# Row sums of a 64 MB array on Trainium2: the first load takes half a row instead of one

## The chip, the cores and the metric

The kernel runs on one core of a Trainium2 chip. The time is device time in microseconds of one execution, from the runs' own clock; where several runs are given, their median stands. The engines that matter are VectorE (DVE in the profile) and ScalarE (ACT), which add, and SyncE (SP), which issues every transfer. The transfers themselves are carried out by 16 DMA engines.

## The reference

```
batch, seq, dim = 32, 512, 1024
x = np.random.randn(batch, seq, dim).astype(np.float32)

def reference(x):
    return np.sum(x, axis=-1).astype(np.float32)
```

There are 32 x 512 = 16384 rows of 1024 floats, 67.1 MB in all. The result is one float for each row, 64 KB.

## The kernel before

**Tiling.** The rows are cut into three blocks that give each of the 128 partitions 32, 48 and 48 consecutive rows (`BLOCKS`, line 10). Within a block, a partition's rows lie one behind the other in memory, so a load of 16 rows is 64 KB of consecutive bytes for every partition. The list `groups` (lines 80 to 88) has seven groups of 16 rows each, 8 MB a group, and the last 16 rows of the last block are loaded in smaller pieces: 9, 4 and 2 rows (`CUTS`) and then the very last row in two parts, of 544 and 480 columns, into the tensor `tail`.

**Buffers.** Three buffers `xt0` to `xt2` (line 37) hold 16 rows for each partition. Group b goes to buffer b modulo 3, and its landing counts on the semaphore `slot0`, `slot1` or `slot2`.

**Loads.** The list `loads` (lines 91 to 101) has every load in its order: buffer, destination, source, semaphore. Group 0 is loaded by two: row 0 with the semaphore `first`, rows 1 to 15 with `slot0` (line 93). Lines 135 to 138 issue them on SP's queue. From group 3 on, SP waits before the issue until VectorE has finished the group that had the buffer before (`freed`).

**Early loads.** At the end (lines 163 to 182) the first two loads (`EARLY`) are taken out of the kernel's body and put into the entry block of SP's program, ahead of the barrier with which all engines start. These are the two loads of group 0.

**Sums.** VectorE waits for `first` (line 106) and then, for each group, for its slot (line 109). `rows_dve` (line 55) is one reduction over 16 rows. In the last group ScalarE takes 7 of the rows (`rows_act`, line 64), and in the pieces about half. The last row is summed by `pairs_dve` (line 72): the two halves of a part are added and accumulated in one instruction.

**Stores.** When the body is done, SP stores three blocks of sums early, and the last 16 columns after the last sum (lines 139 to 147).

Of the kernel before, what the change touches and what calls it, by code (L numbers as in the profile page):

```python
# [11 lines left out]
BUFS = 3  # L12
ACT_ROWS = 7
CUT = 544
CUTS = (0, 9, 13, 15)
EARLY = 2


def row_sums(nc, x: bass.AP, out: bass.AP):
    P = nc.NUM_PARTITIONS  # L20
    x_flat = x.flatten_outer_dims()
    R, D = x_flat.shape
# [4 lines left out]
    xs, outs = [], []  # L27
# [6 lines left out]
    def sbuf(name, n):  # L34
        return nc.alloc_sbuf_tensor(name, [P, n], F32)

    xt = [sbuf(f"xt{i}", G * D) for i in range(BUFS)]
# [9 lines left out]
    sems = {n: nc.alloc_semaphore(n) for n in names}  # L47
    slots = [sems[f"slot{i}"] for i in range(BUFS)]
# [32 lines left out]
    for k, n in enumerate(BLOCKS):  # L81
        c = 0
        end = n - G if k == len(BLOCKS) - 1 else n
        while c < end:
            m = min(G, end - c)
# [4 lines left out]
    freed = {}  # L90
    loads = []
    for b, (k, c, m) in enumerate(groups):
        parts = [(0, m, slots[b % BUFS])] if b else [(0, 1, sems["first"]), (1, m, slots[0])]
        for i, j, s in parts:
            loads.append((b, xt[b % BUFS][:, i * D : j * D], xs[k][:, (c + i) * D : (c + j) * D], s))
    last = xt[n_bufs % BUFS]
    for k, (i, j) in enumerate(zip(CUTS, CUTS[1:])):
        loads.append((n_bufs, last[:, i * D : j * D], x_z[:, (z0 + i) * D : (z0 + j) * D], sems[f"piece{k}"]))
# [18 lines left out]
    for k in range(2):  # L117
        i, j = CUTS[k], CUTS[k + 1]
# [36 lines left out]
def kernel(tc: tile.TileContext, x: bass.AP, out: bass.AP):  # L155
    tc.close()
    tc.compile()  # L157
    nc = tc.nc
    row_sums(nc, x, out)

    sp = mybir.EngineType.SP
    fn = nc.m.functions[0]
    entry, body = None, None
    for blk in fn.blocks:
        ops = [i for i in blk.instructions if i.engine == sp]
        if entry is None:
            entry = blk
        elif any(i.opcode == "DMACopy" for i in ops):  # L170
            body = blk
            break
    code = list(body.instructions)
    loads = [i for i in code if i.engine == sp and i.opcode == "DMACopy"][:EARLY]
    for load in loads:
        assert not load.sync_info.on_wait
        code.remove(load)
    body.instructions = code
    code = list(entry.instructions)
    at = next(k for k, i in enumerate(code) if i.engine == sp and i.opcode == "Drain")  # L180
    code[at:at] = loads
    entry.instructions = code
# [29 lines left out]
```

## Time and profile before

| What | Value |
|---|---|
| Time, median of 3 runs | 160.74 us (160.47 to 160.75) |
| Profiled execution, its own time | 160.68 us |
| Span of that execution in the profile | 159.3 us |
| VectorE busy | 121.4 us |
| ScalarE busy | 17.2 us |
| DMA packets, bytes | 2448, 67.18 MB |
| Mean rate over the span | 422 GB/s |
| One reduction of 16 rows on VectorE | 17.2 us |

Times in the profile count from the start of the span, which is the issue of the first load. A "packet" is what one DMA engine moves at once; here it is one partition's consecutive bytes in one load, and each load has 128 of them, 8 for each of the 16 engines, plus one packet of 4 bytes for each engine that counts on the semaphore. The windows' rates count a packet where it starts, so in short windows with large packets they swing widely; in the first 2 us, where packets are 4 KB, they can be read directly. The difference of 1.4 us between the span and the time of the execution lies before the first and after the last recorded instruction.

### The profile page before, as it was taken

To read this page: it belongs to the slowest core of one execution; us is meant where nothing else is said; L and a number is where in the kernel's file an instruction comes from. 1 tells how busy PE (TensorE), PEld (TensorE's weight loads), DVE (VectorE), ACT (ScalarE), POOL (GpSimd) and SP (SyncE) were. 2 spreads that over 40 slices of the span, in tenths; PEclk is the share of its full clock that TensorE was granted. 3 is DMA by queue.
4 is the path that set the end of the run, shared out by engine and by line. 5 is a ranking of instruction groups with operands and counts; after the bars stand their busy time and mean duration, and the time that the engine had idled before them with its cause. 6 is when DMAs were issued, how large, how long until landed. Compare 5 with 4: busy or idle time off the path is not lost.

```text
span 159.3 us, 109 instructions
## 1 busy us (share of the span) xinstructions
DVE 121.4 (76%) x16; ACT 17.2 (11%) x31; POOL 0.2 (0%) x4
## 2 busy tenths in 40 slices
DVE  0000059998699968999599994999949999499785
ACT  3000000000000000000000000000000000394694
POOL 0000000000000000000000000000000000000000
DMA  9988996996996999979969969969969989699994
GB/s 378 494 386 355 494 526 263 526 510 280 526 494 296 526 395 395 526 329 461 526 280 510 526 263 526 510 280 526 494 296 526 428 362 526 296 444 444 391 409 138
DMA packets 2448, 67.18 MB, mean 422 GB/s; under 512 B 784, under 2 KB 912, under 8 KB 1168
## 3 DMA queue, kind: packets, MB, share of 16 engines
q1 hardware_dynamic: 2448, 67.18, 98.1%
HBM read 67.11 MB, written 0.07 MB: 422 GB/s over the span
## 4 chain that ended last, share of the span: by engine, by line
DMA 75%; DVE 22%; SPq 1%; issue 0%
DMA xt<-in_x_dram 50%; DMA tail<-in_x_dram 25%; DVE res L56 22%; SPq L138 1%; DVE pairs L74 0%; DVE res L74 0%
## 5 line engine op out<-in xcount | busy, mean ns | idle before, releaser
L56 DVE TENSOR_REDUCE res<-xt 128x16 f32<-128x16384 f32 (+3 forms) x9 | 119.8, 13309 | 34.1 <-DMA xt<-in_x_dram 34.1
L67 ACT ACTIVATE xt<-xt 128x1024 f32<-128x1024 f32 x15 | 15.6, 1042 | 138.2 <-DMA xt<-in_x_dram 138.2
L67 ACT ACTIVATION_READ_ACCUMULATOR xt<-xt 128x1 f32 x15 | 2.8, 186 | 0.0
L104 DVE MEMSET tail<- 128x1 f32 x1 | 0.1, 59 | 2.0 <-PEq L157 2.0
L67 ACT ACT_TABLE_LOAD x1 | 1.3, 1283 | 1.9 <-PEq L157 1.9
L74 DVE CUSTOM_DVE_ANT_0 pairs<-tail 128x272 f32<-128x272 f32 (+1 forms) x2 | 0.9, 427 | 0.2 <-DMA tail<-in_x_dram 0.2
L74 DVE CUSTOM_DVE_ANT_0 pairs<-xt 128x512 f32<-128x512 f32 x1 | 0.7, 692 | 0.2 <-DMA xt<-in_x_dram 0.2
L74 DVE DVE_READ_ACCUMULATOR2_ANT res<- 128x1 f32 x2 | 0.2, 82 | 0.0
L196 POOL MEMSET const-bfloat16-1.0<- 128x1 bf16 x1 | 0.1, 102 | 0.0
L196 POOL MEMSET const-uint8-127<- 128x1 uint8 x1 | 0.1, 102 | 0.0
L196 POOL MEMSET const-float32-1.0<- 128x1 f32 x1 | 0.1, 99 | 0.0
L196 POOL MEMSET const-float32-0.0<- 128x1 f32 x1 | 0.1, 98 | 0.2 <-issue 0.2
L74 DVE DVE_READ_ACCUMULATOR2_ANT tail<- 128x1 f32 x1 | 0.1, 83 | 0.0
## 6 DMA issues: line engine op xcount, KB each, us to landing
xt<-in_x_dram SPq DMA_DIRECT2D x1, 7680.0 KB, 21.3
xt<-in_x_dram SPq DMA_DIRECT2D x1, 4608.0 KB, 32.4
xt<-in_x_dram SPq DMA_DIRECT2D x1, 2048.0 KB, 36.9
xt<-in_x_dram SPq DMA_DIRECT2D x1, 1024.0 KB, 38.9
xt<-in_x_dram SPq DMA_DIRECT2D x1, 512.0 KB, 3.5
tail<-in_x_dram SPq DMA_DIRECT2D x1, 272.0 KB, 39.1
tail<-in_x_dram SPq DMA_DIRECT2D x1, 240.0 KB, 39.2
xt<-in_x_dram SPq DMA_DIRECT2D x6, 40.8
```

What stands on the lines that cost most here:

```text
L56: nc.vector.tensor_reduce(out=res[:, c : c + n], in_=t[:, j * D : (j + n) * D].rearrange("p (j d) -> p j d", d=D), axis=X, op=ADD,).then_i ...
L67: nc.scalar.activation(out=v, in_=v, func=COPY, accum_out=res[:, c + i : c + i + 1]).then_inc(act, 1)
L74: nc.vector.tensor_tensor_reduce(out=pairs[:, 0 : h - a], in0=t[:, a:h], in1=t[:, h:b], scale=1.0, scalar=0.0, op0=ADD, op1=ADD, accum_out ...
L104: nc.vector.memset(tail[:, CUT + 15 : CUT + 16], 0.0).then_inc(vec, 1)
L138: nc.sync.dma_start(out=dst, in_=src).then_inc(s, 16)
L196: nc = _bacc.Bacc("TRN2", target_bir_lowering=False, num_devices=1)
```

## The change

A constant `LEAD` of 512 columns is added, and the two loads of group 0 are cut there: the first one brings columns 0 to 511 of row 0 (2 KB for each partition, 256 KB in all) with the semaphore `first`, and the second one brings the rest of row 0 and rows 1 to 15 (62 KB for each partition) with `slot0`. To that end the list's bounds are counted in columns and no longer in rows. All other loads have the same bounds as before.

```
+LEAD = 512
...
     for b, (k, c, m) in enumerate(groups):
-        parts = [(0, m, slots[b % BUFS])] if b else [(0, 1, sems["first"]), (1, m, slots[0])]
+        parts = [(0, m * D, slots[b % BUFS])]
+        if b == 0:
+            parts = [(0, LEAD, sems["first"]), (LEAD, m * D, slots[0])]
         for i, j, s in parts:
-            loads.append((b, xt[b % BUFS][:, i * D : j * D], xs[k][:, (c + i) * D : (c + j) * D], s))
+            loads.append((b, xt[b % BUFS][:, i:j], xs[k][:, c * D + i : c * D + j], s))
```

## The prediction

> **What bounds the kernel now.** I read the page first, its chain and its queue above all, because they say which resource is last. Columns of the transfer rows: size of one, microseconds from issue to landing.
>
> ```profile
> span 159.3 us, 109 instructions
> DVE 121.4 (76%) x16; ACT 17.2 (11%) x31; POOL 0.2 (0%) x4
> q1 hardware_dynamic: 2448, 67.18, 98.1%
> DMA 75%; DVE 22%; SPq 1%; issue 0%
> L56 DVE TENSOR_REDUCE res<-xt 128x16 f32<-128x16384 f32 (+3 forms) x9 | 119.8, 13309 | 34.1 <-DMA xt<-in_x_dram 34.1
> xt<-in_x_dram SPq DMA_DIRECT2D x1, 7680.0 KB, 21.3
> xt<-in_x_dram SPq DMA_DIRECT2D x1, 512.0 KB, 3.5
> ```
>
> The 16 DMA engines are busy for 98.1% of the span; VectorE waits 34.1 us for loads. The 22% that the chain gives to VectorE is buffers being handed back, and that is no stall of the stream: the fourth load is issued when the first reduction ends (39.1 us), while the third load is still in flight until 60 us. So I asked next how evenly the stream runs, by stretches (columns: length, busy time of three engines, clock, share of the 16 DMA engines, GB/s):
>
> ```profile
> 0.90:1.40 0.50, 0.00 (x0) 0.00 (x0) 0.00 (x0) 1.00 0.93 197
> 1.40:1.90 0.50, 0.00 (x0) 0.00 (x0) 0.00 (x0) 1.00 0.90 254
> 1.90:2.40 0.50, 0.06 (x1) 0.49 (x1) 0.00 (x0) 1.00 0.90 360
> 21.00:117.00 96.00, 86.10 (x5) 0.00 (x0) 0.00 (x0) 1.00 1.00 431
> 0.90:157.40 156.50, 120.97 (x14) 17.20 (x31) 0.00 (x0) 1.00 1.00 429
> 155.25:156.50 1.25, 1.04 (x2) 1.25 (x3) 0.00 (x0) 1.00 1.00 386
> ```
>
> From 0.9 to 157.4 us the engines have no hole. The slow stretch is the first microsecond: busy by the record, but at half the rate. The change touches this stretch alone. The queue's own view, cut to two windows that both begin at 0.9 us and end at 1.9 and 2.4 us (packets, MB; share of 16 engines), and the issue of the first two loads on SP's queue (start, length):
>
> ```profile
> q1 hardware_dynamic: 55, 0.23, 91.5%
> ...
> q1 hardware_dynamic: 99, 0.41, 91.1%
> ```
>
> ```profile
> 0.00 0.37 SPq L138 DMA_DIRECT2D xt<-in_x_dram  x1
> ...
> 0.42 0.42 SPq L138 DMA_DIRECT2D xt<-in_x_dram  x1
> ```
>
> The first 55 packets (one is one partition's 4096 bytes) took 0.915 x 16 x 1.0 / 55 = 0.266 us each. The next 44 took (0.911 x 16 x 1.5 - 14.64) / 44 = 0.164 us. The start costs 55 x 0.102 / 16 = 0.35 us per engine, and it is over by about 1.9 us.
>
> **The change part by part.** The number of loads, packets, semaphores and waits stays; SP issues the same two loads first, and nothing is moved past another queue. VectorE waits for `first` and then for `slot0` before its first reduction, as before. That wait ends with the larger load (19.8 us of idle), so an earlier `first` starts nothing. Three costs are left.
>
> 1. Steady price of the packets. Between 60 and 96 us, 233 packets of 64 KB fill 97.9% of 16 engines: 2.420 us each. Against 0.164 us for 4 KB, a byte costs (2.420 - 0.164) / 61440 = 36.7 ps, 2 KB cost 0.075 us, and the rest of a packet is a constant of about 0.014 us. A 2 KB packet is then 0.089 us. The tail's loads (2176 and 1920 bytes per partition), 229 data packets in the 1.25 us that run at 386 GB/s, give 0.995 x 16 x 1.25 / 229 = 0.087 us, so the line holds at this size. Each engine saves 8 x 0.075 = 0.60 us in the first load and pays 8 x 0.075 = 0.60 us in the second one, whose packets grow from 60 to 62 KB. Eight and eight packets remain: sum 0.00 us.
>
> 2. The slow start. Is its 0.35 us charged by the packet, by the byte, or by the clock? If it is a sum for each of the first 55 packets, the same 55 pay it: 0.00. If it is a stretch of time that ends at 1.9 us, packets of 0.089 + 0.102 = 0.191 us let 14.64 / 0.191 = 77 start where 55 did, and 22 x 0.102 / 16 = +0.14 us. If the early packets last 0.266 us whatever their size, 55 of them move half the bytes: 55 x 0.075 / 16 = +0.26 us, and were that to hold for all 128 packets, first-load time would be 128 x 0.266 / 16 = 2.13 us where 55 x 0.266 + 73 x 0.164 over 16 is 1.66; less 0.60 us of bytes taken out, a loss of +1.07. On the other side, an excess in proportion to the packet's size halves: -0.17; and if larger packets following sooner absorbed all of it, -0.35. I take 0.00, between these, because the row of 0.164 us shows that the second half of the row already runs at full rate: the half that is taken out is not the half that suffers.
>
> 3. Cover for the second load. Nothing is free in the first load: its data keep the engines busy until the second load's packets can start. Now the first 60 KB packets start at 2.44 us (the queue's view from 2.4 us on); with 0.60 us less to move, the earliest engine would ask at 1.84. The first load's bytes begin 1.0 us after its issue; the same delay from 0.42 gives 1.42, within the 0.3 us over which engines start, 1.42 to 1.72. The upper bound that the trace allows is 2.44, since it only shows that they could start by then: a hole of up to 0.60 us. I take none, because the delay of the sister load, on the same queue with the same 128 partitions, is the nearest row. Were the cover gone, all 0.60 us would show at the end, since the stream has no hole afterwards in which to catch up.
>
> A rule of the Trainium skill speaks against the change: "DMA: Bandwidth & Descriptors", section "Rules for kernel authors", wants at least 1 MiB in a DMA for full bandwidth, and the new first load has a quarter of that. The trace does not show the loss where a queue is full: the tail's loads of 272 and 240 KB ran at 386 GB/s with the engines 100% busy. By that page's fitted price (section "Bandwidth", 2.0 us plus bytes at 436 GB/s, stated for another issuing path) both cuts sum to the same 4.0 us plus the same bytes, so even the rule gives no difference unless the second fixed part loses its cover. The same page's first-byte latency of about 0.6 us would have the second load ready at 1.02; the trace's own load took 1.0 us.
>
> The end is untouched: the last tail load lands at 157.44, one VectorE operation of 0.41 us and the last store follow. Span and the 1.4 us around it stay. The profiled execution took 160.68 us, 0.06 below the median of 160.74; a sum of 0.00 is 160.7, and I put it at the median, 160.75.
>
> **The rivals.** About 0.2% (0.32 us) is what a measurement of this kernel can tell from no change: the three runs lie 0.28 us apart.
>
> - A hole after the first load (slower). Price min(0.60, time ready - 1.84); it decides beyond the bound when the second load's packets can start only after 2.16 us. For it: each of the neighbouring issues on SP takes 0.37 to 0.42 us and the third and fourth loads are issued at 1.9 and 2.3, so what lies between an issue and its first packet may take longer for a load that follows another closely than the first load alone shows. Against it: 1.42 by the sister load. Time: 160.74 + 0.45 = 161.2 in the middle, 161.34 at most.
> - Early packets at a fixed latency (slower, or just inside the bound): half the bytes in flight, +0.26 us for the first 55 packets, 161.0; if more packets than these stay slow, +0.4 to +1.07. For it: busy engines at half rate, which is what latency with few bytes in flight looks like. Against: nothing shown of smaller packets at the start.
> - The start gets cheaper (faster). The end follows the slowest engine, and the engines do not start alike: the last 4 KB packet starts at 2.97 us, where 60 KB packets began at 2.44, so one engine is 0.5 us behind the first, and nothing later lets it catch up. If the excess goes with the bytes of the first load, the slowest engine has most to gain: -0.35 in the mean, up to -0.5: 160.4 to 160.2.
> - The transfer is hidden anyway: reordering bytes between two back-to-back loads changes nothing, and only the draw of which engine is late moves the time, by about the 0.28 us of the runs. This is the forecast itself.
>
> **How the numbers follow.** No change, cost of the start per packet or short of the bound: 0.44, time 160.6 to 161.0. A hole: 0.17, and a fixed latency or long slow stretch beyond the bound: 0.15; together slower 0.32. A cheaper start: 0.24. I give slower more than faster since its ends reach further (+0.60 and +1.07 against -0.5). The range leaves out the far ends, 0.08 on each side: 160.25 to 161.3. The likeliest case's own range is 160.55 to 160.95.
>
> **What would show it.** Right: 2448 packets again; the second load's first packets near 1.84 us with a full share in the windows on both sides; the 62 KB load landing about 21.3 us after its issue; `tail` landing at 157.4. Step 1 wrong: GB/s between 3 and 21 us differing by more than the shifted bytes. Step 2 wrong: mean packet time in 0.9 to 1.9 us far from 0.19 us. Step 3 wrong: a share of the DMA engines well under 0.9 in a window between 1.7 and 2.5 us, with the landing of the second load and of `tail` later by the same amount. Faster would show as the second load and `tail` landing earlier by equal amounts. What would make the forecast wrong is a start that is charged differently from packet to packet than one trace can show.

## The result and the profile after

The changed kernel takes 160.89 us in the median, the kernel before 160.69 us in the same comparison: a ratio of 1.0015, 95% interval 1.0009 to 1.0021. By that ratio it is 0.24 us more (the medians lie 0.20 us apart), below the 0.2% that the prediction took as its bound; the interval reaches 0.21%. In a second comparison (experiment 5) the ratio was 1.0006, interval 0.9997 to 1.0015, which takes in no change. The two intervals share 0.09 to 0.15%, or 0.14 to 0.24 us.

The page of the changed kernel, its transfer rows with size and microseconds from issue to landing:

```profile
span 159.3 us, 109 instructions
q1 hardware_dynamic: 2448, 67.18, 98.1%
DMA 75%; DVE 22%; SPq 1%; issue 0%
xt<-in_x_dram SPq DMA_DIRECT2D x1, 7936.0 KB, 21.4
xt<-in_x_dram SPq DMA_DIRECT2D x1, 256.0 KB, 2.7
```

Packets, bytes and the share of the DMA engines are those of before. The first load lands 0.8 us sooner after its issue (2.7 instead of 3.5 us), the second one 0.1 us later (21.4 instead of 21.3). Nobody gains from the earlier first landing, as VectorE's first reduction begins at 21.88 us instead of 21.83. The chain of the changed kernel (start, length) shows the same stream:

```profile
1.91 39.22 DMA xt<-in_x_dram
41.15 17.23 DVE res L57
...
118.32 39.10 DMA tail<-in_x_dram
157.42 0.04 issue
157.46 0.41 DVE pairs L75
```

The last load of this execution lands at 157.42 us; before it was 157.44. The profiled execution took 160.67 us and is the fastest of the changed kernel's runs, so it can't show the 0.24 us in its end. It does show what happens at the start. In stretches (length, busy time of three engines, clock, share of the 16 DMA engines, GB/s):

```profile
0.90:1.40 0.50, 0.00 (x0) 0.00 (x0) 0.00 (x0) 1.00 0.59 102
21.00:117.00 96.00, 86.10 (x5) 0.00 (x0) 0.00 (x0) 1.00 1.01 436
0.90:157.40 156.50, 120.94 (x14) 17.21 (x31) 0.00 (x0) 1.00 1.00 429
1.70:2.50 0.80, 0.06 (x1) 0.59 (x1) 0.00 (x0) 1.00 3.70 1423
```

In the first half microsecond half as many bytes start as before (102 instead of 197 GB/s); over the whole stream the rate is 429 GB/s in both. The windows count a packet where it starts, so where packets of 2 and of 62 KB mix, the single records have to be read. The list below is worked out from the packet records of each run's trace, with times in microseconds; the figures are means over the 16 engines, and differences are taken before rounding. "Usual" is how long such a packet takes later in the same load. "Small" is the sum of what one engine's packets of the first load (in the three-load kernels, the first two loads) take beyond their usual time. "Start" is the mean start of the first large packet of each engine, and "extra" what this packet takes beyond the usual. "Loss" is the mean end of group 0, less the mean start of the first packet of all, less the usual time of all packets in between. "Slowest" is when the last of the 16 engines ends its part of group 0, and "time" is the time of this same execution.

```
kernel                      small   first large packet           group 0               execution
                                    start   took  usual  extra   end    loss  slowest  time
one row (before)            0.38    2.76    2.31  2.27   0.04    20.97  0.47  21.42    160.68
half a row (after)          0.18    2.11    2.64  2.34   0.29    21.14  0.61  21.46    160.67
half a row, again (5)       0.31    2.13    2.60  2.34   0.26    21.12  0.62  21.35    161.00
half a row, 4 early (3)     0.26    2.10    2.71  2.34   0.37    21.18  0.71  21.90    161.19
half a row, held (4)        0.21    2.13    2.66  2.34   0.32    21.19  0.68  21.40    160.66
3/4 row (9)                 0.54    2.60    2.32  2.31   0.02    21.13  0.65  21.34    160.64
one row, 4 early (11)       0.72    3.14    2.27  2.27   0.00    21.25  0.72  21.68    160.98
four rows (8)               0.60    6.67    1.81  1.81   0.00    21.17  0.57  21.48    160.83
quarter of a row (2)        0.10    1.93    2.94  2.38   0.56    21.51  1.04  21.83    161.07
single load (1)             -       1.24    3.05  2.42   0.64    21.21  0.62  21.56    160.90
half a row, 1 early (6)     0.32    2.75    2.91  2.34   0.57    22.04  1.54  22.38    161.63
two rows, 1 early (10)      0.58    4.36    2.64  2.12   0.52    22.10  1.50  23.33    162.56
three loads (7)             0.28    3.23    2.90  2.27   0.64    22.65  2.06  24.54    163.82
three loads, held (12)      0.36    3.83    2.75  2.27   0.48    22.74  2.18  23.52    162.76
```

In the kernel before, the small packets of the first load carry the cost of the start. In the changed kernel they carry about half of it, and the rest sits in the first large packet, which takes 2.64 us instead of 2.34. That holds in all four traces with half a row, two loads for group 0 and two or more early loads (0.26 to 0.37 us extra). With one row or three quarters of a row, the extra is at most 0.04 us.

The mean is not what sets the time. The time of an execution less the slowest engine's end is 139.21 to 139.35 us in thirteen of these fourteen executions, and 139.65 in run 5. So they differ almost wholly by when the slowest engine has brought its part of group 0. In run 7 the mean end of group 0 is 1.68 us later than in the kernel before, the slowest engine's end is 3.12 us later, and the execution took 3.14 us more. VectorE's first reduction waits for that engine (start, length; the kernel before, the changed kernel, runs 6, 10 and 7):

```profile
21.83 17.22 DVE L56 TENSOR_REDUCE res<-xt 128x16 f32<-128x16384 f32 x1 [19.79 <-DMA xt<-in_x_dram]
21.88 17.22 DVE L57 TENSOR_REDUCE res<-xt 128x16 f32<-128x16384 f32 x1 [19.84 <-DMA xt<-in_x_dram]
22.81 17.22 DVE L57 TENSOR_REDUCE res<-xt 128x16 f32<-128x16384 f32 x1 [21.25 <-DMA xt<-in_x_dram]
23.78 17.22 DVE L57 TENSOR_REDUCE res<-xt 128x16 f32<-128x16384 f32 x1 [22.21 <-DMA xt<-in_x_dram]
25.02 17.22 DVE L57 TENSOR_REDUCE res<-xt 128x16 f32<-128x16384 f32 x1 [22.50 <-DMA xt<-in_x_dram]
```

In the two profiled executions of the kernel before and the changed one, the slowest engines end 0.04 us apart, and so do not show the loss of the medians.

### The profile page after: what moved, and what is told of

It reads as the page before. It is cut to its first block, busy times and chain, and to the rows that moved or that the text cites. A ratio compares the mean times of both kernels' runs of the same rounds, so it can differ in the third digit from the quotient of the medians.

```text
span 159.3 us, 109 instructions
## 1 busy us (share of the span) xinstructions
DVE 121.4 (76%) x16; ACT 17.2 (11%) x31; POOL 0.2 (0%) x4
## 4 chain that ended last, share of the span: by engine, by line
DMA 75%; DVE 22%; SPq 1%; issue 0%
DMA xt<-in_x_dram 50%; DMA tail<-in_x_dram 25%; DVE res L57 22%; SPq L141 1%; DVE pairs L75 0%; DVE res L75 0%
## 6 DMA issues: line engine op xcount, KB each, us to landing
xt<-in_x_dram SPq DMA_DIRECT2D x1, 7936.0 KB, 21.4
tail<-in_x_dram SPq DMA_DIRECT2D x1, 240.0 KB, 39.1
```

## The experiments

Three theories were set against one another. *Hole*: the second load's packets cannot start before about 1.83 us, and a short first load leaves engines idle. *Clock*: until about 2.4 us engines lose some 0.3 us, whatever they move. *Issues*: the third and fourth issue on SP slow the packets that are in flight. After experiments 1 to 8 a fourth was formed: *cover*. All ratios are to the kernel before on the same chip.

**1. A single load for group 0.** The wait of VectorE on `first` is left out too. As two loads still go out ahead of the barrier, the second of them is now that of group 1.

```
-        if b == 0:
-            parts = [(0, LEAD, sems["first"]), (LEAD, m * D, slots[0])]
...
-    nc.vector.wait_ge(sems["first"], 16)
```

> Group 0 in a single load of 64 KB for each partition, no small load ahead of it (the wait on the small load is gone with it). Theory of the hole (the second load's packets cannot start before about 1.83 us, so a first load that is too short leaves engines idle): there is no second load to wait for, no hole, time at or below the kernel before, 160.4 to 160.75 us. Theory of the clock (until about 2.4 us the engines lose some 0.3 us whatever they move): the first 64 KB packets last about 2.7 us instead of 2.42, time as before, 160.6 to 160.8. Rival, that small packets are needed to get the engines going: 161.0 or more.

Measured: 160.86 us, ratio 1.0005 (0.9997 to 1.0014). The first 64 KB packets took 3.05 us instead of 2.42. Small packets are not needed to get the engines going. The extra of 0.64 us is larger than the clock theory had it, yet the loss is the same as with half a row.

**2. A quarter of a row.**

```
-LEAD = 512
+LEAD = 256
```

> A quarter of a row in the first load (1 KB for each partition). Theory of the hole: the second load still starts at about 1.85 us on the earliest engine, the first load is over by 1.6 to 2.0, so engines idle 0.2 to 0.4 us on average; 8 packets of the second load take 0.038 us more each, +0.30 us, less the 0.1 to 0.2 by which they start sooner: 0.1 to 0.3 us above the changed kernel, 161.0 to 161.2. Theory of the clock alone: as the changed kernel, 160.85 to 160.95. Packets of fixed latency: up to 0.3 us above it.

Measured: 161.02 us, ratio 1.0012 (1.0003 to 1.0021). Here there is a hole: the first load ended at 1.59 us and the first large packets started at 1.93, 0.34 us later, and then took 0.56 us more than usual. The loss, 1.04 us, is the largest of the kernels that issue two loads of group 0 ahead of the barrier. Its median is 0.20 us above the kernel before, and not told apart from the changed kernel.

**3. Four early loads.**

```
-EARLY = 2
+EARLY = 4
```

> The changed kernel with the third and fourth load, too, issued ahead of the barrier (at about 0.9 and 1.3 us instead of 1.9 and 2.3). Theory of the issues (the third and fourth issue slow the packets in flight, and in the changed kernel these are the first 62 KB packets, 2.64 us instead of 2.34): the first 62 KB packets fall to 2.40 us or less, while the 2 KB packets get slower; time 160.6 to 160.8. Theory of the clock: the first 62 KB packets stay near 2.6 us, time as the changed kernel, 160.85 to 160.95.

Measured: 160.70 us, ratio 0.9995 (0.9986 to 1.0004). The first 62 KB packets took 2.71 us, not less: the theory of the issues fails on its own sign. The median is within the range that this theory gave, but the interval takes in no change, and experiment 11 found no gain from the same edit.

**4. The third load held back.**

```
+    nc.vector.memset(xt[2][:, 0 : 8 * D], 0.0).then_inc(vec, 1)
...
+        if n == 2:
+            nc.sync.wait_ge(vec, 2)
```

> The changed kernel with the third load's issue held back until VectorE has cleared half of a buffer that nobody uses yet (some 5 to 10 us), so that SP issues nothing between 0.9 and that time; the stream cannot run dry before 20 us. Theory of the issues: the first 62 KB packets last 2.34 to 2.40 us instead of 2.64, and the time falls to 160.6 to 160.75. Theory of the clock: they stay near 2.6 us, 160.85 to 160.95.

Measured: 160.85 us, ratio 1.0001 (0.9993 to 1.0010). From the timeline of this run (start, length), the clearing that SP waited for:

```profile
3.72 6.88 DVE L108 MEMSET xt<- 128x8192 f32 x1 [1.68 <-issue]
```

SP issued nothing between 0.9 and 10.6 us, and the first 62 KB packets still took 2.66 us. So the issues are not the cause of the slow packets. The median is the clock theory's figure, but its interval takes in no change and overlaps that of the changed kernel.

**5. The changed kernel again.**

> The changed kernel once more, so that the four kernels of this set have it beside them on the same chip. Both theories: 0.1 to 0.25 us above the kernel before; first 62 KB packets about 2.6 us, second load's packets from about 1.83 us on.

Measured: 160.93 us, ratio 1.0006 (0.9997 to 1.0015); first 62 KB packets 2.60 us, the earliest at 1.91 us. The packets are as expected; the loss is at the lower end, and its interval takes in no change.

**6. One early load.**

```
-EARLY = 2
+EARLY = 1
```

> The changed kernel with only the first load ahead of the barrier; the second one is issued behind it, at about 1.9 us instead of 0.42, so that its packets start at 2.8 to 3.1 us, 0.8 us later than in the changed kernel, into idle engines. Theory of the clock (packets that start before about 2.4 us are slow, whichever they are): the first 62 KB packets last 2.34 to 2.40 us, and the time is 0.8 - 0.29 = 0.5 us above the changed kernel, 161.3 to 161.5. Rival, that the first large packet of an engine pays wherever it starts unless enough small ones ran before: they last about 2.6 us, and the time is 0.8 us above, 161.6 to 161.8.

Measured: 161.83 us, ratio 1.0060 (1.0043 to 1.0076). The second load was issued at 1.43 us, sooner than I had expected, and its packets started from 2.40 us on. Two windows of this run, the first holding the 16 first large packets alone, the second the 16 next ones (packets, MB, share of 16 engines):

```profile
DMA packets 16, 1.02 MB, mean 1026 GB/s; under 512 B 0, under 2 KB 0, under 8 KB 0
q1 hardware_dynamic: 16, 1.02, 293.8%
```

```profile
DMA packets 16, 1.02 MB, mean 1665 GB/s; under 512 B 0, under 2 KB 0, under 8 KB 0
q1 hardware_dynamic: 16, 1.02, 384.8%
```

The windows are 0.99 and 0.61 us long. The first gives 2.938 x 16 x 0.99 / 16 = 2.91 us for a packet, the second 3.848 x 0.61 = 2.35. Packets that start between 2.40 and 3.38 us are slow, so a loss that ends at about 2.4 us, the clock theory, is not the cause. The rival's range (161.6 to 161.8) was passed by 0.03 us.

**7. Three loads.** Half a row, half a row, 15 rows, all ahead of the barrier (`EARLY = 3`; VectorE waits for the added semaphore `half` as well).

```
-            parts = [(0, LEAD, sems["first"]), (LEAD, m * D, slots[0])]
+            parts = [(0, LEAD, sems["first"]), (LEAD, D, sems["half"]), (D, m * D, slots[0])]
```

> Group 0 in three loads: half a row, the other half, 15 rows, all three issued ahead of the barrier. The same bytes as in the kernel before run in small packets, 16 of 2 KB instead of 8 of 4 KB for each engine, and the large packets have 60 KB again and start at 2.5 to 2.9 us. Theory of the clock: the small packets take the slow stretch, the first 60 KB packets last 2.27 to 2.35 us, time as the kernel before plus about 0.08 us for eight more packets and a count for each engine. Rival, that the half row itself (packets of 2 KB at the start) costs: 0.2 us or more above the kernel before. Rival, that a hole is what costs: the third load's packets cannot start before 2.3 us, no hole, as the kernel before.

Measured: 163.29 us, ratio 1.0141 (1.0120 to 1.0161). No theory had this. Pages of this run, and its timeline on SP's queue:

```profile
q1 hardware_dynamic: 2592, 67.18, 96.9%
...
xt<-in_x_dram SPq DMA_DIRECT2D x1, 7680.0 KB, 24.0
xt<-in_x_dram SPq DMA_DIRECT2D x2, 256.0 KB, 2.8
```

```profile
2.39 1.61 SPq L142 DMA_DIRECT2D xt<-in_x_dram  x2
```

The load of 15 rows, issued at 0.90 us, lands 24.0 us after its issue; in the kernel before the same load took 21.3. Its first packets are slow and so are the second ones (2.83 us instead of 2.27), up to about 9 us. The fifth issue alone lasted 1.23 us.

**8. Four rows first.**

```
-LEAD = 512
+LEAD = 4096
```

> Four rows in the first load (16 KB for each partition), twelve in the second. Theory of the clock: the 16 KB packets that start before 2.4 us (the first two of each engine) take the whole loss; the total is what large packets lose there (the half row lost 0.14 us more per engine than the row, a single 64 KB load as much): 0.1 to 0.2 us above the kernel before. Theory of the hole alone: no hole, as the kernel before or better.

Measured: 160.79 us, ratio 0.9997 (0.9989 to 1.0006). The first 16 KB packets took 1.20 us where 0.61 is usual, the second ones 0.62, and the 48 KB packets of the second load had no extra at all. The loss sits in the first packet of each engine. As the second packets started at 2.40 us in the mean, this run alone can't tell that from a stretch of time that ends at about 2.4 us; run 6 can.

The theory of *cover* came from these. In every run so far with two loads for group 0 and a short first one, the large packets ran at their usual rate as if they had started at "start" plus "extra": 2.41, 2.39, 2.47 and 2.45 us with half a row (changed kernel, 5, 3, 4), 2.49 with a quarter, 3.31 in run 6; the single load 1.88. Less the issue of that load (0.42 to 0.43 us; 1.43 in run 6; 0 for the single load) this is 1.88 to 2.06 us each time. What the first load's packets do not fill until then would be lost. One row fills until 2.75 us, half a row until 2.05.

**9. Three quarters of a row.** `LEAD = 768`.

> Three quarters of a row first (3 KB for each partition). Theory of cover (a load of large packets moves at full rate only 1.9 to 2.05 us after its issue, so the second one, issued at 0.42, from about 2.42 on; what the first load's packets do not fill until then is lost, partly as a gap and mostly inside the record of the first large packet): the first load fills until 1.48 + 8 x 0.121 = 2.45 us on average, which just covers; first large packets about 0.05 to 0.12 us above their usual 2.305 us (half of the engines are done sooner than the average), time between the kernel before and the changed one, 160.8 to 160.85. Rival, that the first large packets pay by the size of what ran before (4 KB +0.04, 2 KB +0.29, 1 KB +0.56): about +0.17 us, 160.85 to 160.95.

Measured: 160.73 us, ratio 0.9994 (0.9984 to 1.0004). The first large packets started at 2.60 us with 0.02 us extra: the cover is complete, as that theory says, and the rival's +0.17 us is excluded. The small loss of time that the theory expected (160.8 to 160.85 us) did not show, and the mean loss of 0.65 us is no smaller than with half a row.

**10. Two rows first, one early load.** `LEAD = 2048`, `EARLY = 1`.

> Two rows in the first load (8 KB for each partition) and only this load ahead of the barrier, so that the second one is issued at about 1.43 us, as in the run with half a row that took 161.83 us. Theory of cover: the second load flows at 1.43 + 1.9 to 2.0 = 3.35 to 3.45 us; the first load's packets, which start to flow at about 1.5 to 1.8, last 8 x 0.309 = 2.5 us, until 4.0 to 4.3, so all is covered: first packets of 56 KB at their usual time within 0.05 us, time 160.7 to 161.0. Rival, that a second load issued behind the barrier costs by itself, or that each load's first packet pays wherever it stands: 161.4 to 161.9.

Measured: 161.81 us, ratio 1.0069 (1.0047 to 1.0091). The theory of cover fails here. The small packets filled until 4.25 us, 2.8 us after the second load's issue, and still its first packets took 0.52 us more than usual, and the others of the load 0.28 us in sum (the second ones 2.38 us instead of 2.12). Stretches of this run, with the columns as above:

```profile
1.00:4.00 3.00, 0.06 (x1) 1.28 (x1) 0.00 (x0) 1.00 0.97 333
4.00:9.00 5.00, 0.00 (x0) 0.00 (x0) 0.00 (x0) 1.00 1.08 398
9.00:21.00 12.00, 0.00 (x0) 0.00 (x0) 0.00 (x0) 1.00 1.03 444
```

The slow stretch reaches beyond 4 us. The mean loss is that of run 6 (1.50 and 1.54 us), which had one early load and half a row, and so is the median time: the cover of the first load bought nothing. The parts differ, though: run 6 has a gap of 0.65 us between the two loads' packets, run 10 one of 0.11 us. The profiled execution of run 10 was the longest of its four, with its slowest engine 0.95 us behind that of run 6.

**11. The kernel before with four early loads.** `EARLY = 4`, one row first.

> The kernel before with four loads ahead of the barrier instead of two. The changed kernel with four came out at 0.9995 of the kernel before. Theory of cover: the third and fourth load are not needed before 20 us, so their issue changes nothing: 0.999 to 1.001 of the kernel before. Rival, that issues behind the barrier slow the packets in flight at 1.9 to 2.7 us: 0.1 to 0.2 us faster than before.

Measured: 160.83 us, ratio 0.9998 (0.9989 to 1.0007): no change. This run's trace has 0.00 us extra on the first 60 KB packets and 0.72 us on the small ones, where the kernel before had 0.38. The medians agree, so this difference of 0.25 us between two single executions is taken for their scatter. The one of run 11 was also the longest of its eleven.

**12. Three loads, the fourth held back.** Run 7 with the holding back of run 4, ahead of the fourth load.

> The three loads of group 0 (half row, half row, 15 rows) issued ahead of the barrier as in the run that took 163.29 us, with the fourth load's issue held back until VectorE has cleared half of an unused buffer, some 10 us. If the loss of 2.5 us comes from the fourth and fifth load being issued (at 2.4 and 2.8 us, the fifth issue took 1.23 us) on top of the three in flight: it goes, 160.8 to 161.0, and the first 60 KB packets last 2.27 to 2.40 us. If it comes from two loads of small packets ahead of the large one: it stays, 163 to 163.5, with the first two 60 KB packets at about 2.9 us.

Measured: 163.18 us, ratio 1.0146 (1.0127 to 1.0165). The loss of the three loads stays without any further issue, so the fourth and fifth load do not cause it. The load of 15 rows started its packets 1.00 us after the small ones were done (at 3.83 us in the mean, 2.94 us after its issue), and again lost 0.48 us in the first of them. Its transfer rows:

```profile
xt<-in_x_dram SPq DMA_DIRECT2D x1, 7680.0 KB, 23.0
xt<-in_x_dram SPq DMA_DIRECT2D x2, 256.0 KB, 2.8
```

No kernel was clearly faster than the kernel before. Three quarters of a row (0.9994) and four early loads with half a row (0.9995) have intervals that take in 1.

## Why the prediction was right, and where its steps were not

The time, 160.89 us, lies in the range of 160.25 to 161.3 and in the own range of the likeliest case, 160.55 to 160.95. The forecast was no change within 0.2%; the loss of 0.15% is on the side that was given more weight.

*What bounds the kernel* was right. The stream fills all 16 engines from 1 us to 157.4 us, and nothing later gives back what the start loses: in run 6 a second load issued 1.0 us later made the kernel 0.9 us slower than the changed kernel of the same set (161.83 against 160.93 us). (The load issued at 39.1 us, which the prediction calls the fourth, is the fifth in the list; the argument does not change.)

*Step 1, the steady price of the packets*, was right. Later 62 KB packets took 2.34 us and 60 KB packets 2.27, 0.075 us apart as worked out; a 2 KB packet took 0.084 us for an estimate of 0.089. The sum of 0.00 holds.

*Step 2, the slow start*, took the charge as a sum for each packet, with the same packets paying as before. That reading failed: the small packets' own excess fell from 0.38 us to 0.18 (0.21 to 0.31 in the other three runs with half a row), and the first large packet took over 0.26 to 0.37 us. The sign that was set for it, a mean packet time far from 0.19 us between 0.9 and 1.9 us, says the same: the 97 packets of 2 KB that started then took 0.114 us. The total per engine came out as the step had it, nearly unchanged: 0.61 to 0.71 us in four traces with half a row, 0.47 to 0.72 in three with one row or three quarters. Runs 1 and 8 show why the term balances: the first packets of each engine pay about 0.6 us in sum at the start of the stream, whether they have 16 or 64 KB.

*Step 3, cover for the second load*, took 1.42 us for the time from which the second load's packets could start, by the delay of the first load, with 2.44 as the upper bound. In the record the earliest large packet did start at 1.83 us, when its engine was nearly done (1.84 was forecast), and the mean gap was 0.06 us in the changed kernel's trace and 0.01 in run 5. So there was almost no hole between packets. With a quarter of a row the earliest large packet started at 1.52 us, within the 1.42 to 1.72 us of the step, and the mean one at 1.93. But counted back from their ends, the first large packets behaved as if the full rate had come only at about 2.4 us, near the upper bound: the loss lies inside their records. The step's error was to take a packet that has started for one that moves at full rate. The sign that was set for it, a share well under 0.9, could not catch this, as a packet counts in full where it starts (3.70 between 1.7 and 2.5 us). The price was not the 0.60 us of the rival: gap and extra together are 0.35 us in the mean, and the first load's packets lost 0.20 us less than before. That these errors of steps 2 and 3 have opposite signs and left about 0.15 us was not worked out beforehand; there the number is right partly by luck.

*The rival of the hole* decides only with a shorter first load: a quarter of a row has a gap of 0.34 us. *Early packets at a fixed latency* is refuted for small packets: from the second one on, the 2 KB packets of the changed kernel took 0.09 us and not 0.27. *The cheaper start* did happen in the small packets and was used up in the large ones; its premise, that the end follows the slowest engine, held in thirteen of the fourteen traces.

Two details of the prediction were off. The price of 2.0 us plus bytes at 436 GB/s stands on the Trainium skill's page "DMA: Bandwidth & Descriptors" in the section "Anatomy of one DMA — SWDGE (gpsimd) path", not in "Bandwidth". And the tail's 386 GB/s, read as no loss, is a tenth below the 431 GB/s of the large loads.

What stays open: the traces do not resolve the 0.24 us between the two kernels. Their mean losses of 0.47 and 0.61 us differ, but run 11 (0.72 with one row) shows that one trace can't carry this, and the slowest engine, which sets the time, ends only 0.04 us later. That the extra in the first large packet is what makes the changed kernel slower is argued from four traces and from the order of the runs with a quarter, a half and three quarters of a row; it is not shown. Nor is it known why one engine starts slower than the others, or what makes large packets slow at their start. The clock (run 6) and the issues (runs 3, 4) are out as its only cause. Cover explains the runs with two early loads and fails where a later issue was covered (run 10) and with three loads (runs 7, 12).

## What to carry to other kernels

Here transfers fill the whole time, and a resized first load touches the start of the stream alone. Anything from half a row to four rows stayed within 0.2% by the ratios, as did no small load at all. A packet that has started may still be slow (2.64 us instead of 2.34): look whether the first packets of a load last longer than the later ones before a gap of zero is read as a cost of zero. Look at the slowest engine beside the mean, as the time followed it. The issue of the load that the stream needs next had to go out early and behind one small load at most: behind the barrier it cost 0.6%, and as a third load 1.4%.

## What the hardware showed that I had not expected

- The first packets of each engine lose about 0.6 us together at the start of the stream, with little regard to their size: 16 KB packets took 1.20 us instead of 0.61, 64 KB packets 3.05 instead of 2.42.
- Cutting one row out of group 0 into two halves, with the same bytes, made the kernel 2.5 us slower than one row did (163.29 us against 160.80), and holding back all further issues did not help (163.18 us). In the first of these two kernels the large packets behind ran at about 80% of their rate for two rounds (2.90 and 2.83 us instead of 2.27; 2.75 and 2.48 in the second).
- With the second load issued 1.0 us later, the kernel took about 1.0 us more than the kernel before, whether the first load had half a row (161.83 against 160.80 us) or two rows (161.81 against 160.87 us), although two rows kept the engines busy until 4.25 us.
- The time of an execution followed the slowest of the 16 engines at the end of group 0, and not their mean: the time less that end was 139.21 to 139.35 us in thirteen of fourteen traces, although these ends lie between 21.34 and 24.54 us.
